# Reordering evictions, moving two norms and packing narrow products in a one-core encoder step

## The chip, the core and the metric

The kernel runs on one core of one Trainium2 chip. The core has a matrix engine (TensorE, "PE" in the profile, with its weight loads as "PEld"), VectorE ("DVE"), ScalarE ("ACT"), GpSimd ("POOL") and SyncE ("SP"), which issues nearly all of the kernel's DMAs. Each engine works through its own queue in order. The metric is the device time of one execution in microseconds (us); lower is better.

## What is computed

One layer of a streaming encoder, for a prompt of 2048 tokens and for a decoding batch of 8 sequences of 16 tokens (128 rows), both through the same weights. Width 1024, all in float32:

```python
qm, km, vm, om, ip, fp, qa, ka, va = split_in(x @ w_in)
hm, C1, n1, m1 = mlstm_chunkwise(qm, km, vm, logi, logf, C0, n0, m0, mchunk)   # 4 heads x 128
hm = og * head_norm(hm, g_mlstm_norm)
ha = swa_prompt(rope(qa), rope(ka), va, sinks)   # batch: swa_step, with a cache of 128 rows
mix = jnp.concatenate([hm, ha], axis=-1) @ w_out
h = layer_norm(DEEPNORM_ALPHA * x + mix, ln1_g, ln1_b)
u = h @ w_up                                     # 5632 columns: value | gate
c = b_conv + sum(ext[:, j:j + T] * w_conv[j] for j in range(CONV_W))
f = (silu(g) * a) @ w_down
y = layer_norm(DEEPNORM_ALPHA * h + f, ln2_g, ln2_b)
```

The mLSTM keeps a matrix state C and a vector n for each head; a token's numerator is the inner product within its chunk plus its query times the state. The prompt starts from C = 0; each of the 8 batch sequences brings its own state. The new states, the last keys and values and the last convolution rows are outputs too.

## The kernel before

The 2048 prompt tokens are 16 tiles of 128 rows (tiles 0 to 15); the batch is tile 16. Large products are made at near float32 accuracy from single-pass products: each operand is split into a high part (a cast on ACT, L217 for weights, L564 for tokens) and a low part (a subtraction on DVE, L218 and L565), and three products high x high, high x low, low x high are summed in PSUM. Blocks of the matrices are combined by a seven-product scheme of Strassen's kind, so a "step" s is one of seven products, and each step ends in an eviction out of PSUM that copies or adds. The splits for later steps run some steps ahead of their products.

PE's instructions run in exactly the order in which the program writes them. For the other engines and the DMA queues a planner fixes the order at compile time: from estimated durations it goes through a simulated time and gives each engine, of what is ready, the instruction with the highest priority, by default the one that the program wrote first. What the planner has put in a queue then runs in that order on the chip.

There are four stages in time.

1. **Input projection** (`i_dense`, to about 650 us). For four blocks of tiles and five column groups it runs `i_product` (L702, steps), `i_direct` (L728, gates, keys and values) and after each step `i_after`, which evicts (L769 on ACT, L773 and L775 on DVE are typical) and, through `i_out`, applies the rotary angles (`rope`, four DVE operations, L866 to L869, in group 2) and stores the result. `advance` then issues loads and splits for weights. Small chains are woven between the dense products: the batch (`t_sample`, `swa_sample`), the prompt's mLSTM tile by tile (`m_chain`, `m_tile`) and its attention (`a_chain`, `swa`). A chain is a generator: `yield cost, wait, banks` tells the weaver how much PE time its last part takes and how many ns of PE time are to pass before its next part is written into PE's stream. That wait is the lead which the chain's DVE, ACT and DMA work gets. `m_rows` sends gate rows through DRAM to all partitions (`wi<-zM`), and `m_tile` masks them on DVE (L1106).
2. **Output projection** (`o_block`, five blocks: tiles 16,0,1 / 2-5 / 6-9 / 10-13 / 14,15). An eviction adds the product to alpha * x (L1610), and the finished tile gets its first layer norm by the generator `norm` (statistics at L1564 and L1554, then two DVE operations over 1024 columns, L1568 and L1570, and the store to `zh`). The norms of one block advance on every second product of the next. Within the last block the up-projection already begins: `f_hT(0)` loads and transposes normed tiles (L1698), `f_tokens` splits them, `f_next` splits weights. The norms of the last block's own tiles 14 and 15 are made later, in the up-projection, by `o_late`.
3. **Up-projection** (`f_ups`, about 920 to 1861 us). Three blocks of tiles, 22 column pairs j each, seven steps (L1834). `f_after` does a step's eviction (L1851 to L1870) and, after steps 3 and 4, the convolution (L1882 on ACT, L1884 on DVE), the gate and the stores. `o_late` advances at steps 6 and 5 from j = 2 on; `f_hT` for the next block starts at j = 6 and advances at the same steps.
4. **Down-projection** (`f_downs`, to the end). Products at L2039; `add` evicts (L2066, L2068), then the second norm and the output.

For the batch, `t_sample` multiplies each head's queries with 8 states: per head 8 products of 128 stationary columns, of which only one sequence's 16 are not zero (`qm` holds them on a block diagonal, L1436), against 129 columns of state (L1439). `swa_sample` handles the 8 sequences in two halves; a half's products with the cached values (L1525) and the new values (L1526) go, for each of two kv heads, into a bank of 64 partitions, and each bank is evicted by itself (L1527).

Of the kernel before, what the change touches and what calls it, by code (L numbers as in the profile page):

```python
# [14 lines left out]
P = 128  # L15
# [189 lines left out]
class Prog:  # L205
# [380 lines left out]
    def i_dense(self):  # L586
# [34 lines left out]
        for item in self.items:  # L621
# [39 lines left out]
            behind = self.i_after(b, g, s)  # L661
# [378 lines left out]
    def m_chain(self):  # L1040
        nc = self.nc
        while not self.chains.done["s"]:
            yield 0, 500
        load = self.m_next = None
        for t in range(NPT):
            b, ti = self.place(t)
            while self.i_done <= b:
                yield 0, 500
            load = load or self.m_load(t, b, ti)
            if self.m_next is None:  # L1050
                self.m_next = self.m_rows(t, b, ti)
# [12 lines left out]
        nc.sync.dma_start(self.a["m_p"], self.mc)  # L1064
        nc.sync.dma_start(self.a["cn_p"], self.C)
# [116 lines left out]
    def m_tile(self, t, load):  # L1182
# [61 lines left out]
    def a_chain(self):  # L1244
# [115 lines left out]
    def t_sample(self):  # L1360
# [49 lines left out]
        qm = [self.work("sc", [P, DB * P], bufs=2, name="qm") for i in range(2)]  # L1410
# [16 lines left out]
        for j in range(2):  # L1427
            ps = self.bank([P, 2, 129], "pnum")
            for i in range(2):
# [5 lines left out]
                dg = bass.AP(q.tensor, q.offset, [list(q.ap[0]), [P + DS, DB], [1, DS]])  # L1435
                V.tensor_copy(dg, b3(qw[:, h]))  # L1436
                nc.tensor.matmul(ps[:, i], sd[:, h], v1[:, h], start=True, stop=False)
                for bb in range(DB):
                    nc.tensor.matmul(ps[:, i], q[:, bb * P:(bb + 1) * P], cn[:, bb], start=False, stop=bb == DB - 1)  # L1439
# [7 lines left out]
                yield 4000, 3500  # L1447
# [21 lines left out]
    def swa_sample(self, load, kvc):  # L1469
# [15 lines left out]
        for half in range(2):  # L1485
# [35 lines left out]
            for kvh in range(2):  # L1521
                po = self.bank([64, HB, 64], "ppo")
                cs = slice(64 * kvh, 64 * kvh + 64)
                for b in range(HB):
                    nc.tensor.matmul(po[:, b], vc[:, b, cs], pts[:, 0, b, cs], start=True, stop=False)  # L1525
                    nc.tensor.matmul(po[:, b], vn[:, b, cs], pts[:DS, 1, b, cs], start=False, stop=True)  # L1526
                (V.tensor_copy if kvh else nc.scalar.copy)(  # L1527
                    mix[cs].rearrange("p j (b l) -> p j b l", b=DB)[:, :, bs], po.rearrange("p b (j l) -> p j b l", j=4))
            if half == 0:
                kvc = self.swa_cache(1)  # L1530
            yield 1900, 500 if half else 7000
# [54 lines left out]
    def o_block(self, b):  # L1586
# [7 lines left out]
        for hf in range(2):  # L1594
            c = slice(hf * 512, hf * 512 + 512)
            steps = 0
            for cost, ti, ps in self.group(b, tiles, 8 * b + 4 * hf, hf == 1):
# [12 lines left out]
                nc.vector.scalar_tensor_tensor(y[:, c], ys[ti][:, c], ALPHA, ps, op0=ALU.mult, op1=ALU.add)  # L1610
                if hf and b < nb - 1:
# [11 lines left out]
    def o_late(self):  # L1623

        nc, V = self.nc, self.nc.vector
        st = []
        for y, t in self.late:
            st.append(self.stats(y))
            yield
        for hf in range(2):  # L1630
            c = slice(hf * 512, hf * 512 + 512)
            gb = self.f3.tile([P, 2, 512], F32, name="lnp", tag="th", bufs=1)
            for i, n in enumerate(("ln1_g", "ln1_b")):
                nc.sync.dma_start(gb[:, i], self.a[n][:, c].to_broadcast([P, 512]))
            yield
            yield
            for (y, t), (mv, s) in zip(self.late, st):
                V.scalar_tensor_tensor(y[:, c], y[:, c], mv[:, 0:1], gb[:, 0], op0=ALU.subtract, op1=ALU.mult)
                V.scalar_tensor_tensor(y[:, c], y[:, c], s[:, 0:1], gb[:, 1], op0=ALU.mult, op1=ALU.add)
                if hf:  # L1640
                    nc.sync.dma_start(self.zh[t], y)
                yield

# [135 lines left out]
    def f_ups(self, n):  # L1779
# [11 lines left out]
        for i, (b, j, s) in enumerate(self.seq):  # L1791
            if s == 6 and j == 6 and b + 1 < nb:
# [13 lines left out]
            if b + 1 < nb and j == NFF - 1:  # L1806
                if s == 1:
# [28 lines left out]
    def f_after(self, b, j, s):  # L1836
# [11 lines left out]
        m = WP - h  # L1848
        half = lambda v: f2.tile([P, 770], F32, name=f"u{v}", tag=f"u{v}", bufs=1)
# [19 lines left out]
        elif s == 4:  # L1869
            V.tensor_add(self.ug[:, 2:2 + h], C, self.u2[j % 2])  # L1870
        if s not in (3, 4):
            return

# [132 lines left out]
    def f_downs(self):  # L2006
# [35 lines left out]
        def after(s, p):  # L2042
            ps = banks[role[s][2 if p == np_ else p]]
            ta, tb = (tiles[2 * np_], None) if p == np_ else (tiles[p], tiles[np_ + p])
            if s == 1:
                S.copy(banks[role[6][2 if p == np_ else p]], ps)
# [16 lines left out]
        def add(t, half, ps, first):  # L2063
            y = ys[t][:, half * 512:half * 512 + 512]
            if first:
                V.scalar_tensor_tensor(y, y, ALPHA, ps, op0=ALU.mult, op1=ALU.add)  # L2066
            else:
                V.tensor_add(y, y, ps)  # L2068
# [71 lines left out]
```

## Time and profile before

| | |
|---|---|
| median of 3 runs | 2336.47 us (2332.86 to 2341.85) |
| profiled execution | 2337.74 us, of which the span from the first to the last instruction is 2336.0 us |
| mean granted TensorE clock | 0.992 of full speed |
| DMA | 629.24 MB, mean 269 GB/s |

| stretch, us | stage | PE busy | DVE busy | ACT busy |
|---|---|---|---|---|
| 0 to 900 | input and output projection | 883.90 | 688.12 | 537.87 |
| 900 to 940 | last output block, start of the up-projection | 35.02 | 39.68 | 23.19 |
| 940 to 1860 | up-projection | 916.13 | 706.60 | 511.48 |
| 1860 to 2336 | down-projection | 465.46 | 384.26 | 202.66 |

A row of the timeline gives the start in us, the duration, engine, line, operation, "out<-in", for a matmul the size of its stationary operand (128*128) and of its moving one (128x256), and the count; in brackets stands the idle time of the engine before it and what ended that. The row of an x2 or x4 covers that many instructions up to the last one's end. A matmul's duration contains its way through the array, so the distance of two starts tells what it costs in a stream. The page's busy time counts an engine as busy while any of its instructions is under way, at whatever clock.

### The profile page before, as it was taken

The numbers are of one execution on the slowest core, as the hardware profiler recorded it, in microseconds if no ns is written. First come the engines' busy times: TensorE is split into PE (matmuls) and PEld (weight loads), VectorE is DVE, ScalarE is ACT, GpSimd is POOL, SyncE is SP. The second block draws the span as 40 slices with busy tenths as digits, with TensorE's granted clock in tenths as the row PEclk, the third lists the DMA queues.
The fourth block names the chain that finished last, engine by engine and source line by source line (L and its number), as shares of the span: only waits on it lengthen the run. The fifth ranks groups of instructions, "written<-read, shape, count | busy, mean of one in ns | idle before, by whom it ended". The sixth has DMA issues, their size and how long they took to land. (4 is left out here: it accounts for less than half of the span.)

```text
span 2336.0 us, 39880 instructions
## 1 busy us (share of the span) xinstructions
PE 2300.5 (98%) x14301; PEld 2112.0 (90%) x14301; DVE 1818.7 (78%) x3187; ACT 1275.2 (55%) x2409; POOL 253.0 (11%) x477
## 2 busy tenths in 40 slices
PE   8999999999999999999999999999999999999998
PEld 8999989998987777999999999999999978888876
DVE  7786587797688888988788776778766786896987
ACT  5453457776766664556556555556554544444452
POOL 0001000000011111211102010102111200100100
PEclk9999999999999999999999999999999999999999
DMA  7888889989987766788777889878998786756753
GB/s 271 293 304 294 285 271 337 318 291 330 327 274 251 233 214 250 268 319 295 265 275 267 311 310 318 304 266 279 308 299 262 224 288 197 258 175 226 251 157 108
DMA packets 298727, 629.24 MB, mean 269 GB/s; under 512 B 47709, under 2 KB 140961, under 8 KB 298529
## 3 DMA queue, kind: packets, MB, share of 16 engines
q1 hardware_dynamic: 294144, 612.99, 76.7%
q0 software_dynamic: 3520, 10.56, 1.4%
q10 hardware_dynamic: 864, 3.15, 0.3%
q8 instruction: 113, 1.85, 0.3%
q14 instruction: 86, 0.70, 0.1%
HBM read 456.01 MB, written 170.59 MB: 268 GB/s over the span
## 5 line engine op out<-in xcount | busy, mean ns | idle before, releaser
L1834 PE MATMUL fup<-hh,uw 128*128 128x384 f32 (+1 forms) x1848 | 480.7, 329 | 2.5 <-DVE uw L218 2.1
L1834 PE MATMUL dps<-hh,uw 128*128 128x384 f32 (+1 forms) x1848 | 478.7, 328 | 3.4 <-DVE u L1864 2.4
L1834 PEld LDWEIGHTS fup<-hh,uw 128*128 128x128 f32 x1848 | 331.6, 189 | 3.7 <-DVE uw L218 2.4
L1834 PEld LDWEIGHTS dps<-hh,uw 128*128 128x128 f32 x1848 | 330.2, 188 | 4.2 <-DVE u L1864 2.7
L1884 DVE SCALAR_TENSOR_TENSOR cc<-u,cw,cc 128x768 f32<-128x768 f32 (+1 forms) x264 | 258.4, 979 | 63.8 <-ACT cc L1882 57.6
L1834 PE MATMUL fup<-hl,uw 128*128 128x384 f32 (+1 forms) x924 | 303.7, 329 | 2.6 <-DVE hl L218 2.5
L1834 PE MATMUL dps<-hl,uw 128*128 128x384 f32 (+1 forms) x924 | 302.5, 327 | 0.0
L702 PE MATMUL dps<-w,oh 128*128 128x256 f32 x1344 | 257.2, 286 | 1.3 <-DVE zev L775 0.8
L217 ACT CAST uw<-wraw 128x1024 fp32r<-128x1024 f32 x126 | 123.0, 979 | 225.5 <-PE dps L2039 119.9
L218 DVE TENSOR_TENSOR w<-wraw,w 128x1024 fp32r<-128x1024 f32 (+2 forms) x167 | 189.0, 1139 | 55.4 <-ACT w L217 54.3
L217 ACT CAST w<-wraw 128x1024 fp32r<-128x1024 f32 (+2 forms) x167 | 162.9, 983 | 119.1 <-PE dps L702 57.1
L702 PEld LDWEIGHTS dps<-w,oh 128*128 128x128 f32 x1344 | 212.5, 189 | 12.8 <-issue 8.9
L218 DVE TENSOR_TENSOR uw<-wraw,uw 128x1024 fp32r<-128x1024 f32 x126 | 142.3, 1131 | 66.2 <-ACT uw L217 66.0
L702 PE MATMUL dps<-w,ol 128*128 128x256 f32 x672 | 188.8, 281 | 0.0
L1834 PEld LDWEIGHTS fup<-hl,uw 128*128 128x128 f32 x924 | 174.5, 189 | 3.3 <-DVE hl L218 3.2
L2039 PE MATMUL fup<-uw,fu 128*128 128x512 f32 x726 | 174.5, 396 | 1.7 <-DVE uw L218 1.7
L702 PE MATMUL dps<-oh,w 128*128 128x256 f32 x896 | 170.7, 285 | 5.3 <-ACT zev L769 3.2
L1834 PEld LDWEIGHTS dps<-hl,uw 128*128 128x128 f32 x924 | 173.6, 188 | 0.0
L2039 PEld LDWEIGHTS fup<-uw,fu 128*128 128x128 f32 x726 | 136.8, 189 | 35.2 <-DVE uw L218 2.1
L2039 PE MATMUL dps<-uw,fu 128*128 128x512 f32 x660 | 165.2, 395 | 1.1 <-DVE uw L218 1.1
L1882 ACT ACTIVATE cc<-u,cw 128x768 f32<-128x768 f32 (+1 forms) x132 | 132.2, 1002 | 56.4 <-DVE u L1870 30.0
L702 PEld LDWEIGHTS dps<-oh,w 128*128 128x128 f32 x896 | 142.0, 191 | 11.9 <-issue 4.1
(323 smaller groups left out, 4594.7 us busy)
## 6 DMA issues: line engine op xcount, KB each, us to landing
uw<-zw SPq DMA_DIRECT2D x176, 512.0 KB, 5.3
zw<-uw SPq DMA_DIRECT2D x88, 512.0 KB, 2.9
w<-zws SPq DMA_DIRECT2D x72, 512.0 KB, 6.4
wv<-wup SPq DMA_DIRECT2D x66, 512.0 KB, 4.5
wraw<-wi SPq DMA_DIRECT2D x65, 512.0 KB, 5.1
wraw<-zt SPq DMA_DIRECT2D x60, 512.0 KB, 4.2
wraw<-wdn SPq DMA_DIRECT2D x45, 512.0 KB, 4.1
wraw<-wo SPq DMA_DIRECT2D x40, 512.0 KB, 4.8
```

What stands on the lines that cost most here:

```text
L217: nc.scalar.copy(hi, src)
L218: nc.vector.tensor_sub(lo, src, hi.bitcast(F32))
L702: mm(o, l, r, start=s in (1, 7) and c == k == i == 0, stop=k == 3 and i == 2, skip_group_check=True)
L1834: mm(ps, l[:, k], r[:, k], start=s in (1, 7) and k == 0 and i == 0, stop=k == 3 and i == 2, skip_group_check=True)
L1882: S.activation(c[:, v], u[:, 2:2 + n], AF.Identity, bias=w[3], scale=w[2])
L1884: V.scalar_tensor_tensor(c[:, v], u[:, i:i + n], w[i], c[:, v], op0=ALU.mult, op1=ALU.add)
L2039: mm(ps, l[:, k, c], r[:, k], start=s in (1, 4, 7) and u == 0 and k == 0 and i == 0, stop=u == nu - 1 and k == n - 1 and i == 2, skip_grou ...
```

## The change

Six edits:

1. **Priority.** The evictions of the input projection (all of `i_after`), of the output projection (L1610), of the up-projection (cut out of `f_after` as `f_evict`) and of the down-projection (`add`, and the copy of step 1) are written inside `high_priority()`: the planner takes them before any other instruction that is ready on that engine. PE's order is not touched by it.
2. **Longer leads.** At the first tile of an input block the mLSTM chain waits 15000 ns instead of 12000 after `m_rows`, the attention chain 9000 instead of 4500 after its load.
3. **Tile 0** of the prompt leaves out the product with the state C, which is zero there.
4. **State products of the batch.** The block diagonal `qm` shrinks from 128 to 32 columns per sequence; pairs of sequences share a group of 32 output partitions, and the loop goes over the four groups in turn. The part's cost is given as 2800 ns instead of 4000.
5. **Value products of the batch.** Both kv heads of a half go to one bank of 128 partitions, in neighbouring instructions, with one eviction. Cost 1000 instead of 1900.
6. **Norms of tiles 12 and 13.** Their un-normed rows are stored to `zh` at once; `o_late`, after tiles 14 and 15, loads them again, norms them and stores them. `o_late` advances at steps 6, 5 and 7, and `f_hT` of the next block starts at j = 12 instead of 6.

```diff
-            behind = self.i_after(b, g, s)
+            with self.tc.high_priority():
+                behind = self.i_after(b, g, s)
...
-                yield 150, 12000, 1
+                yield 150, 15000, 1
...
-                nc.tensor.matmul(ps[:, i], sd[:, h], v1[:, h], start=True, stop=False)
-                nc.tensor.matmul(ps[:, i], qk[:, h], self.C[:, h], start=False, stop=True)
+                nc.tensor.matmul(ps[:, i], sd[:, h], v1[:, h], start=True, stop=t == 0)
+                if t:
+                    nc.tensor.matmul(ps[:, i], qk[:, h], self.C[:, h], start=False, stop=True)
...
-                yield 0, 4500
+                yield 0, 9000
...
-                dg = bass.AP(q.tensor, q.offset, [list(q.ap[0]), [P + DS, DB], [1, DS]])
-                V.tensor_copy(dg, b3(qw[:, h]))
-                nc.tensor.matmul(ps[:, i], sd[:, h], v1[:, h], start=True, stop=False)
-                for bb in range(DB):
-                    nc.tensor.matmul(ps[:, i], q[:, bb * P:(bb + 1) * P], cn[:, bb], start=False, stop=bb == DB - 1)
+                dg = bass.AP(q.tensor, q.offset, [list(q.ap[0]), [64, DB // 2], [32 + DS, 2], [1, DS]])
+                V.tensor_copy(dg, qw[:, h].rearrange("p (c b l) -> p c b l", b=2, l=DS))
+                nc.tensor.matmul(ps[:, i], sd[:, h], v1[:, h], start=True, stop=False, skip_group_check=True)
+                for r in range(2):
+                    for c in range(DB // 2):
+                        nc.tensor.matmul(ps[32 * c:32 * c + 32, i], q[:, 2 * c + r], cn[:, 2 * c + r], start=False, stop=r == 1, skip_group_check=True)
...
-            for kvh in range(2):
-                po = self.bank([64, HB, 64], "ppo")
-                cs = slice(64 * kvh, 64 * kvh + 64)
-                for b in range(HB):
-                    nc.tensor.matmul(po[:, b], vc[:, b, cs], pts[:, 0, b, cs], start=True, stop=False)
-                    nc.tensor.matmul(po[:, b], vn[:, b, cs], pts[:DS, 1, b, cs], start=False, stop=True)
...
+            po = self.bank([P, HB, 64], "ppo")
+            for b in range(HB):
+                for i, (v, p) in enumerate(((vc[:, b], pts[:, 0, b]), (vn[:, b], pts[:DS, 1, b]))):
+                    for kvh in range(2):
+                        cs = slice(64 * kvh, 64 * kvh + 64)
+                        nc.tensor.matmul(po[cs, b], v[:, cs], p[:, cs], start=i == 0, stop=i == 1, skip_group_check=True)
...
+                if hf and b == nb - 2 and ti >= len(tiles) - 2:
+
+                    nc.sync.dma_start(self.zh[tiles[ti]], y)
+                elif hf and b < nb - 1:
                     self.norms.append(self.norm(y, *self.ln1, self.zh[tiles[ti]]))
...
+        for late in (self.late, OBLOCKS[-2][-2:]):
+            if late is not self.late:
+                late = [(self.fp.tile([P, D], F32, name="ymix", tag="hst", bufs=2), t) for t in late]
+                for y, t in late:
+                    nc.sync.dma_start(y, self.zh[t])
+                for _ in range(3):
+                    yield
...
-            if s == 6 and j == 6 and b + 1 < nb:
+            if s == 6 and j == 12 and b + 1 < nb:
...
+            with self.tc.high_priority():
+                self.f_evict(b, j, s)
             self.f_after(b, j, s)
...
-            if j >= 2 and s in (6, 5):
+            if j >= 2 and s in (6, 5, 7):
                 next(late, None)
...
+            with self.tc.high_priority():
+                if first:
+                    V.scalar_tensor_tensor(y, y, ALPHA, ps, op0=ALU.mult, op1=ALU.add)
+                else:
+                    V.tensor_add(y, y, ps)
```

More of the change, by code (lines that the diff above doesn't have):

```diff
@@ L1409, in t_sample @@
         states = [state(h) for h in range(2)]
-        qm = [self.work("sc", [P, DB * P], bufs=2, name="qm") for i in range(2)]
+        qm = [self.work("sc", [P, DB, 32], bufs=2, name="qm") for i in range(2)]
         for q in qm:
@@ L1446, in t_sample @@
                 vws = weighted(h + 1) if h + 1 < MH else None
-                yield 4000, 3500
+                yield 2800, 3500
             num.append(ps)
@@ L1609, in o_block @@
                 y = outs[ti]
-                nc.vector.scalar_tensor_tensor(y[:, c], ys[ti][:, c], ALPHA, ps, op0=ALU.mult, op1=ALU.add)
-                if hf and b < nb - 1:
+                with self.tc.high_priority():
+                    nc.vector.scalar_tensor_tensor(y[:, c], ys[ti][:, c], ALPHA, ps, op0=ALU.mult, op1=ALU.add)
+                if hf and b == nb - 2 and ti >= len(tiles) - 2:
+                    nc.sync.dma_start(self.zh[tiles[ti]], y)
+                elif hf and b < nb - 1:
                     self.norms.append(self.norm(y, *self.ln1, self.zh[tiles[ti]]))
@@ L1625, in o_late @@
         nc, V = self.nc, self.nc.vector
[L1626 to L1641, printed above, removed]
-                yield
+        for late in (self.late, OBLOCKS[-2][-2:]):
[5 more added lines that the diff above has]
+                    yield
+            st = []
+            for y, t in late:
+                st.append(self.stats(y))
+                yield
+            for hf in range(2):
+                c = slice(hf * 512, hf * 512 + 512)
+                gb = self.f3.tile([P, 2, 512], F32, name="lnp", tag="th", bufs=1)
+                for i, n in enumerate(("ln1_g", "ln1_b")):
+                    nc.sync.dma_start(gb[:, i], self.a[n][:, c].to_broadcast([P, 512]))
+                yield
+                yield
+                for (y, t), (mv, s) in zip(late, st):
+                    V.scalar_tensor_tensor(y[:, c], y[:, c], mv[:, 0:1], gb[:, 0], op0=ALU.subtract, op1=ALU.mult)
+                    V.scalar_tensor_tensor(y[:, c], y[:, c], s[:, 0:1], gb[:, 1], op0=ALU.mult, op1=ALU.add)
+                    if hf:
+                        nc.sync.dma_start(self.zh[t], y)
+                    yield
     def f_setup(self):
@@ L1806, in f_ups @@
             if b + 1 < nb and j == NFF - 1:
+                if s == 1 and b == 0:
+                    assert next(late, self) is self
                 if s == 1:
@@ L1848, in f_after @@
         m = WP - h
+        self.fshape = n, WP, has_s, sam
         half = lambda v: f2.tile([P, 770], F32, name=f"u{v}", tag=f"u{v}", bufs=1)
@@ L1870, in f_after @@
             V.tensor_add(self.ug[:, 2:2 + h], C, self.u2[j % 2])
+    def f_after(self, b, j, s):
         if s not in (3, 4):
             return
+        nc = self.nc
+        V, S = nc.vector, nc.scalar
+        n, WP, has_s, sam = self.fshape
         v, u = (0, self.uv) if s == 3 else (1, self.ug)
@@ L2045, in after @@
             if s == 1:
-                S.copy(banks[role[6][2 if p == np_ else p]], ps)
+                with self.tc.high_priority():
+                    S.copy(banks[role[6][2 if p == np_ else p]], ps)
             elif s == 2:
@@ L2064, in add @@
             y = ys[t][:, half * 512:half * 512 + 512]
[L2065 to L2068, printed above, removed]
+            with self.tc.high_priority():
+                if first:
+                    V.scalar_tensor_tensor(y, y, ALPHA, ps, op0=ALU.mult, op1=ALU.add)
+                else:
+                    V.tensor_add(y, y, ps)
         def finish(t, b, step):
```

7 lines of the change are left out of this document (3 added, 4 removed).

## The prediction

> **What bounds the kernel now.** Read first the page: the span and the busy time of each engine.
>
> ```profile
> span 2336.0 us, 39880 instructions
> PE 2300.5 (98%) x14301; PEld 2112.0 (90%) x14301; DVE 1818.7 (78%) x3187; ACT 1275.2 (55%) x2409; POOL 253.0 (11%) x477
> ```
>
> TensorE (PE) is idle for 35.5 us in all. No reordering of other engines can win more than that, except in two ways: PE gets fewer or cheaper matmuls, or its clock stays up. So the second view is the timeline of PE alone, for rows that carry idle time before them. After the first 50 us these are the ones that bear on this change (start, duration, engine, line, operation; in brackets the idle time and what ended it):
>
> ```profile
> 306.45 0.56 PE L728 MATMUL dps<-w,oh 128*128 128x264 f32 x2 [2.23 <-DVE zev L775]
> 334.27 0.58 PE L702 MATMUL dps<-oh,w 128*128 128x256 f32 x1 [2.49 <-ACT zev L769]
> 472.86 0.52 PE L728 MATMUL dps<-w,oh 128*128 128x264 f32 x2 [1.51 <-DVE zev L775]
> 584.16 0.39 PE L702 MATMUL dps<-w,oh 128*128 128x256 f32 x1 [0.78 <-DVE zev L775]
> 923.25 0.62 PE L1834 MATMUL fup<-hh,uw 128*128 128x384 f32 x2 [2.10 <-DVE uw L218]
> 933.92 0.44 PE L1834 MATMUL fup<-hl,uw 128*128 128x384 f32 x1 [2.49 <-DVE hl L218]
> 1588.34 0.44 PE L1834 MATMUL dps<-hh,uw 128*128 128x384 f32 x1 [0.60 <-DVE u L1862]
> 1858.70 0.42 PE L1834 MATMUL dps<-hh,uw 128*128 128x320 f32 x1 [2.44 <-DVE u L1864]
> ```
>
> Six of the eight wait for an eviction (L769, L775, L1862, L1864): DVE or ACT had other work in front. The other two wait for a split (L218). The third view is the table of stretches, because a stall can cost twice. Columns: stretch, length, then busy time of PE, PEld, DVE, ACT, POOL with instruction counts, then PEclk (granted clock, 1.00 is full), DMA share, GB/s.
>
> ```profile
> 262.60:266.00 3.40, 3.40 (x17) 2.81 (x18) 0.42 (x1) 0.00 (x0) 0.00 (x0) 0.50 0.39 137
> 266.00:269.40 3.40, 3.40 (x18) 3.40 (x18) 0.69 (x1) 1.18 (x2) 0.00 (x0) 0.52 0.23 76
> ...
> 286.50:289.90 3.40, 3.40 (x29) 2.73 (x28) 3.37 (x4) 2.54 (x5) 0.00 (x0) 1.00 0.93 285
> ...
> 306.90:310.40 3.50, 3.50 (x19) 3.50 (x19) 3.50 (x4) 1.05 (x1) 0.00 (x0) 0.53 0.72 224
> ...
> 334.30:337.70 3.40, 3.40 (x17) 3.40 (x18) 0.68 (x1) 1.33 (x2) 0.00 (x0) 0.53 0.97 346
> ...
> 474.80:478.20 3.40, 3.40 (x31) 3.40 (x30) 3.40 (x7) 3.02 (x5) 0.00 (x0) 1.00 0.66 212
> ...
> 924.80:928.20 3.40, 3.40 (x12) 3.40 (x12) 3.40 (x6) 0.46 (x1) 0.00 (x0) 0.53 0.71 286
> ...
> 935.00:938.40 3.40, 3.40 (x12) 3.31 (x11) 3.40 (x4) 2.66 (x6) 0.00 (x0) 0.52 0.52 203
> ...
> 1860.00:1863.40 3.40, 3.40 (x12) 2.93 (x11) 3.40 (x6) 0.93 (x1) 0.00 (x0) 0.52 0.52 181
> ```
>
> The reader is to see that after each idle time of 2.1 us or more the clock is granted at half for the next 3.4 us, and PE, though "busy", does half the work: 3.4 x 0.47 = 1.6 us lost. After the 1.51 us before 472.86 it stays at 1.00. So a stall of 2.1 us or more really costs 1.6 us more than it shows. The stretch from 262.6 has no idle time at all; it comes behind narrow matmuls, below.
>
> **Part 1: less and denser PE work.** The trace records each f32 product twice.
>
> ```profile
> 198.88 1.95 PE L1439 MATMUL pnum<-cns,qm 128*128 128x129 f32 x16
> 200.67 1.90 PE L1443 MATMUL pcs<-vws,kw 128*128 128x387 f32 x6
> ...
> 259.66 0.33 PE L1525 MATMUL ppo<-pts,kvc 128*64 128x64 f32 x2
> ...
> 264.10 0.47 PE L1526 MATMUL ppo<-pts,vn 16*64 16x64 f32 x2
> ...
> 287.71 0.33 PE L1525 MATMUL ppo<-pts,kvc 128*64 128x64 f32 x2
> ...
> 291.55 0.32 PE L1526 MATMUL ppo<-pts,vn 16*64 16x64 f32 x2
> ```
> ```profile
> 350.12 0.65 PE L1349 MATMUL ppo<-pth,kva 128*64 128x512 f32 x2
> 350.60 0.60 PE L1349 MATMUL ppo<-pth,kva 128*64 128x512 f32 x2
> ```
> ```profile
> 274.57 0.44 PE L1498 MATMUL pscs<-kvc,qs 64*64 64x128 f32 x4
> 274.84 0.25 PE L1499 MATMUL pscs<-ks,qs 64*64 64x16 f32 x4
> 274.93 0.43 PE L1498 MATMUL pscs<-kvc,qs 64*64 64x128 f32 x4
> ```
>
> The batch's state products (L1439) take 200.67 - 198.88 = 1.79 us a head, 16 records at 0.112. Tile 0's product with the zero state C has the same shape and goes: four heads, two records each, 8 x 0.112 = 0.9 us.
>
> L1439's become 16 records of 32 columns in four column groups. If nothing overlaps, nothing is gained; if all four do, 1.79 / 4 = 0.45 is left. That groups overlap here is shown by L1349: two 64-column products start together, and the next two 0.48 us later. The nearest row for a pace is L1498: from 274.57 to 274.93 eight records (four of L1498, four of L1499) go, 0.045 us each. 16 x 0.045 = 0.72, and up to 0.26 for changing the array's shape before and after (no more than a whole product of L1525 takes, next paragraph): about 1.0. Saving 0.8 x 4 = 3.2 us; ends 0 and 5.4.
>
> The attention's L1525/L1526 took 287.71 to 291.81 = 4.1 us in the second half: 16 products in turn, (291.55 - 287.71) / 15 = 0.26 each, alternating between 128 and 16 rows. In the first half it was 259.66 to 264.50 = 4.8. Now both kv heads go to one bank, 64 columns each, with two products to every change of rows: 8 steps. I take 0.27 for a step, since L1349 shows pairs side by side: 2.2 us per half. Saving 2.6 + 1.9 = 4.5; none if a pair runs in turn. Of the two evictions one is left, off the path.
>
> The clock goes with it. From 259.66 to 262.6 there were 2.9 us of narrow products and the clock fell; the second half put 2.2 us of them into 286.5 to 289.9 and it didn't. 2.2 us is all that is left of a half, so the fall goes: 264.5 to 269.4 at half is 2.4 us. Part 1: 0.9 + 3.2 + 4.5 + 2.4 = **11.0 us**.
>
> The Trainium skill ("TensorE: Matmul & The Clock Gate", Part 3, on what overlaps) speaks against some of this: matmuls start and end strictly in program order. Then a product's second record would hold back the next group's first, and a head would need 8 x 0.112 + 0.26 = 1.2 us, an attention step about 0.05 more: 1.6 us less saved, 2313 in place of the forecast below. The L1349 rows speak for pairs that start together, if the two started together are of different groups, which no column tells.
>
> **Part 2: evictions first, longer leads, in the input projection.** 2.23 + 2.49 + 1.51 + 0.78 = 7.0 us of idle time and two clock falls, 3.2 us. What stood in front of the first:
>
> ```profile
> 303.97 0.69 DVE L1106 TENSOR_TENSOR dt<-k_mcau,wi 128x512 f32<-128x512 f32 x1 [3.00 <-DMA wi<-zM]
> 304.58 1.22 DVE L565 TENSOR_TENSOR ol<-xr,oh 128x1024 fp32r<-128x1024 f32 x1
> ...
> 305.72 0.68 DVE L775 TENSOR_TENSOR zev<-dps,zev 128x512 f32<-128x512 f32 x1
> ```
>
> DVE, in order, sat 3.00 us on a mask whose broadcast had not landed, then did a split of 1.22 us, then the eviction. The lead of 15000 in place of 12000 moves the mask 3 us back, which is as long as it waited; the priority moves the split behind L775. Only one of the two is needed to bring this stall under 2.1 us. I take three quarters of the idle time, 5.3 us, and both falls: **8.5 us**; at most 10.2. The lead of 9000 for the attention's load acts once per input block; what it adds lies beside dense products, whose count is the same.
>
> **Part 3: two norms moved.**
>
> ```profile
> 898.75 0.69 DVE L1554 BATCH_NORM_STATS2 lst<-ymix 128x6 f32<-128x512 f32 x1
> ...
> 901.20 1.27 DVE L1568 SCALAR_TENSOR_TENSOR ymix<-ymix,lmv,o_ln_g 128x1024 f32<-128x1024 f32 x1
> ...
> 902.91 1.28 DVE L1570 SCALAR_TENSOR_TENSOR ymix<-ymix,lsc,o_ln_b 128x1024 f32<-128x1024 f32 x1 [0.31 <-POOL lsc L1557]
> ```
> ```profile
> 910.00:920.00 10.00, 10.00 (x45) 8.11 (x44) 10.00 (x11) 3.04 (x4) 0.00 (x0) 1.00 0.52 159
> ```
>
> A norm is 2 x 0.69 + 1.27 + 1.28 = 3.9 us of DVE, two are 7.9. DVE has no free moment from 910 on, so what follows comes up to 7.9 us sooner; the stalls at 923 and 934 want 2.10 and 4.6 together. Both go with their falls: 4.6 + 3.2 = 7.8. I take **7 us**, as some splits also wait for transposes. The moved norms bring two stores, two loads and four parameter loads on SP's queue, three yields behind their issue, and the same DVE time some 50 to 150 us later. Up to each moment DVE has then been given no more work than before, so its backlog isn't larger. The transposes of block 1 start six steps later and still end before the last step needs them. If this cover failed, 7.9 us would come back.
>
> **Part 4: evictions first, later stages.**
>
> ```profile
> 1856.82 0.89 DVE L1884 SCALAR_TENSOR_TENSOR cc<-u,cw,cc 128x656 f32<-128x656 f32 x1
> ```
>
> This and a split stood before L1862 and L1864 of the last step, from 1856.8 to 1858.1. Going first saves 1.3 of the 2.44 us, and the fall (1.6). With 0.5 of the 0.60 at 1588: **3.4 us**. In the down-projection the same priority finds little idle time to win.
>
> **Sum.** 11.0 + 8.5 + 7 + 3.4 = 29.9 us. Parts 2 to 4 redraw the order of DVE, ACT and SP; an order planned from estimates meets the chip with stalls of its own. I give back a quarter of their 19: 5 us. 25 us off the profiled execution's 2337.74 is 2312.7; the median of the runs shown is 1.3 below it: **2311.5**.
>
> **Rivals.**
> 1. The stalls only move: other splits or masks become late as L775 is served, and parts 2 and 4 net nothing. For it: the eight waits have five different releasers, so they look like chance. Against: PE waits for evictions in six. 11 + 7: 2318.5.
> 2. It doesn't do what it says: 32- and 64-column products still run in turn. Part 1 shrinks to 0.9, and the clock falls again: 25 - 10.1 = 14.9, so 2321.6. L1349 speaks against it. If the stalls move as well, only 0.9 + 7 is left: 2328.6.
> 3. Slower: the priority covers all of i_after, so the rotary work too, and splits wait for it.
>
> ```profile
> 250.79 0.42 DVE L866 TENSOR_TENSOR rb<-zev,ropet 128x256 f32<-128x256 f32 x1
> ...
> 251.65 0.69 DVE L868 TENSOR_TENSOR zev<-zev,ropet 128x512 f32<-128x512 f32 x1
> ```
>
> One rotary pass is 2 x 0.42 + 2 x 0.69 = 2.2 us of DVE, 16 passes (four per block in group 2) are 35 us. It decides where splits are less than 2.2 us ahead of their products. If all were, with parts 1 and 3 still won, 2336.5 + 35 - 18 = 2353. Against it: in the steady stretch PE waits for evictions, not for w.
>
> **How the numbers follow.** Forecast 0.55 (own range 2303 to 2320), rival 1 0.20, rival 2 0.10, rival 2 with moved stalls 0.08, rival 3 0.07. All gains at their upper ends and nothing given back reach 2301; with rivals 1 and 2 taken in the range is 2301 to 2327. A measurement tells 0.5% (11.7 us, 2324.8) from no change. Faster 0.78, within 0.15, slower 0.07.
>
> **What would show it.** L1439's line at 1.0 us a head; the two attention stretches at 2.2 us with PEclk 1.00 behind them; no idle time of 2 us or more at L702, L728 and L1834; DVE free time before 920. It would be wrong if PE's idle time came out near 35 us again, or if waits for w or uw by L218 grew.

## The result, and the profile after

| kernel | median | runs | ratio to the kernel before |
|---|---|---|---|
| before | 2335.15 us | 6 | |
| changed | 2322.59 us (2317.53 to 2328.13) | 6 | 0.9943 [0.9927, 0.9959] |
| changed, once more (e11) | 2321.53 us (2321.05 to 2324.56) | 5 | 0.9942 [0.9928, 0.9955] |

The change is worth 0.57%, 12.6 us, with the whole interval below 1: faster, but by half of the 25 us that were forecast. 2322.59 lies in the prediction's range of 2301 to 2327, which takes rivals 1 and 2 in, but not in the forecast's own, 2303 to 2320. Two rows of the changed kernel's page say where to look:

```profile
span 2322.7 us, 39853 instructions
...
PE 2287.1 (98%) x14293; PEld 2095.7 (90%) x14293; DVE 1818.9 (78%) x3189; ACT 1274.3 (55%) x2409; POOL 261.3 (11%) x477
```

PE's idle time is 2322.7 - 2287.1 = 35.6 us; before it was 35.5. So the part of the change that was meant to remove waits removed none in sum. All of the gain is in PE's busy time, 2300.5 - 2287.1 = 13.4 us. PE has 8 instructions less, the eight records of tile 0's product with the zero state; the rest of the 13.4 us are products that take less time, because they are narrower or because the clock stays up. From 20 us on to the down-projection's end, the profiled execution of before has eight windows of 3.41 us at half clock, that of the changed kernel three.

The waits are still there, at other places. These are the rows of PE's timeline in the changed kernel with the longest idle time ahead of them behind the first 50 us (columns as before):

```profile
329.79 0.58 PE L703 MATMUL dps<-oh,w 128*128 128x256 f32 x1 [3.56 <-ACT mr L1151]
...
685.92 1.53 PE L1345 MATMUL ppt<-ident,sc 128*128 128x128 f32 x6 [1.47 <-ACT sc L1323]
...
919.84 0.49 PE L1853 MATMUL fup<-hl,uw 128*128 128x384 f32 x1 [2.50 <-DVE hl L218]
...
1846.64 0.41 PE L1853 MATMUL dps<-hh,uw 128*128 128x320 f32 x1 [1.99 <-DVE u L1884]
...
1890.91 6.33 PE L2065 MATMUL fup<-uw,fu 128*128 128x512 f32 x26 [1.63 <-DVE uw L218]
```

The first row comes in place of the stalls at 306.45 and 334.27 of before, some 13 us further on in the stream than the second of them, and is longer than either. The one at 923.25 is gone, the one at 933.92 stays as 919.84 with the same 2.5 us, and the one at 1858.70 became 1.99. The wait of 1.47 us at 685.92 is new. The last row is no new one: the kernel before waits 1.66 us at the same place.

What stood ahead of the first stall is on DVE's timeline of the changed kernel, then on ACT's:

```profile
324.69 0.69 DVE L849 TENSOR_TENSOR txy<-txy 128x512 f32<-128x512 f32 x1 [3.45 <-DMA txy<-wdn]
325.30 0.29 DVE L1148 BATCH_NORM_STATS2 bst<-pnum 128x6 f32<-128x128 f32 x1
```
```profile
328.12 0.17 ACT L1151 ACTIVATE mr<-pnum 128x2 f32<-128x2 f32 x1 [2.69 <-DVE bst L1148]
328.20 1.04 ACT L217 CAST w<-wraw 128x1024 fp32r<-128x1024 f32 x1
329.15 0.59 ACT L770 ACTIVATE zev<-dps 128x512 f32<-128x512 f32 x1
```

DVE sat 3.45 us at the head of its queue on a load of the down-projection's weights (`wdn`, for sums that are made ahead of time). The mLSTM chain's statistics came late by that; ACT, in order as well, sat 2.69 us on them; and the eviction L770, which is now marked to go first, came out at 329.15, behind them and a cast. (The row of PE names the next `mr` on ACT; L770 ends at 329.74 and that one at 329.80, after PE has started.) This is the picture of before with other names: one engine waits at the head of its queue for a load, and PE waits at the end of the row.

To see where the 13 us arise, each of the 12097 dense matmuls of the changed kernel was laid beside the one with the same number in the kernel before. What the changed kernel gains on each stretch (times of before, us):

| stretch | what lies there | gained |
|---|---|---|
| 0 to 45 | start; a half-clock stretch at 40.5 is missing | 2.0 |
| 45 to 193 | steady input projection | -1.3 |
| 193 to 237 | state products of the batch | 4.0 |
| 237 to 297 | value products, and the clock behind them | 6.3 |
| 297 to 341 | stalls at 306 and 334 with their half clock, tile 0's product | 7.2 |
| 341 to 358 | the changed kernel's own stall at 329.79 and its half clock | -5.6 |
| 358 to 650 | rest of the input projection | 1.9 |
| 650 to 903 | output projection: new stall and half clock at 686 | -4.5 |
| 903 to 952 | start of the up-projection, moved norms | 4.1 |
| 952 to 1841 | up-projection | -2.5 |
| 1841 to 1882 | last step of the up-projection | 2.0 |
| 1882 to the end | down-projection | -0.3 |

The packed products give 4.0 + 6.3 and tile 0's 0.9, 11.2 us; the norms 4.1; all the rest comes to -2.0. From about 300 to 470 us the chains stand at other places between the dense products, and the gain swings by up to 2.6 us from product to product; of the three rows from 297 to 650 only the sum, 3.5 us, is firm.

The table compares two executions, and some rows hold chance. e9 below has all six edits, and its clock is at half again from 40.7 us on, so the first 2.0 us are not the change's. e11 is the changed kernel once more: the same wait of 1.47 us in the output projection brings no half clock there, while its wait at the last step of the up-projection, 1.99 us as here, brings one there and none here.

The timeline of PE around the batch's products in the changed kernel:

```profile
198.00 0.38 PE L1440 MATMUL pnum<-v,sd 128*128 128x129 f32 x2
198.31 0.65 PE L1443 MATMUL pnum<-cns,qm 128*32 128x129 f32 x16
198.89 2.00 PE L1447 MATMUL pcs<-vws,kw 128*128 128x387 f32 x6
...
255.58 0.34 PE L1531 MATMUL ppo<-pts,kvc 128*64 128x64 f32 x4
...
257.42 0.33 PE L1531 MATMUL ppo<-pts,vn 16*64 16x64 f32 x4
```

The 16 records of a head now take 198.89 - 198.31 = 0.58 us in the stream, against 1.79. The products ahead of them and behind them take 0.2 us more together than before (from 198.00 to 198.31 it is 0.31 us, where it was 0.22), so a head saves 1.0 us. A half of the value products has eight steps, (257.42 - 255.58) / 7 = 0.263 us each, 2.1 us in all, against 4.8 and 4.1. And the clock, in the table of stretches of the changed kernel (columns as in the prediction):

```profile
254.50:257.90 3.40, 3.40 (x44) 2.72 (x42) 1.56 (x2) 1.30 (x3) 0.00 (x0) 1.00 0.92 344
257.90:261.30 3.40, 3.40 (x31) 3.40 (x31) 0.69 (x1) 1.45 (x3) 0.00 (x0) 1.00 0.76 213
```

It stays at 1.00 behind the narrow products, where it was 0.50 and 0.52 before.

### The profile page after: what moved, and what is told of

The parts are those of the page before. It is cut to its first block, busy times and chain, and to the rows that moved or that the text cites. A ratio compares the mean times of both kernels' runs of the same rounds, so it can differ in the third digit from the quotient of the medians.

```text
span 2322.7 us, 39853 instructions
## 1 busy us (share of the span) xinstructions
PE 2287.1 (98%) x14293; PEld 2095.7 (90%) x14293; DVE 1818.9 (78%) x3189; ACT 1274.3 (55%) x2409; POOL 261.3 (11%) x477
```

## The experiments

Four theories went into them. **A**: the gain is the packing's and part of the norms'; the priority and the leads move stalls and remove none. **B**: the priority removes waits, as forecast. **C**, formed after the first four: packing pays only with the attention chain's longer lead. **D**, formed for e7: the stalls that are left come from the written order, a load of down-projection weights issued too shortly ahead of its sums, and weight sums of the up-projection written ahead of the split `hl`; writing these differently takes the waits away. None of the kernels leaves out part of the computation; e9 makes one product three times.

**e1: the packing alone** (edits 3, 4 and 5 in the kernel before; the core of it):

```diff
-                    nc.tensor.matmul(ps[:, i], q[:, bb * P:(bb + 1) * P], cn[:, bb], start=False, stop=bb == DB - 1)
+                        nc.tensor.matmul(ps[32 * c:32 * c + 32, i], q[:, 2 * c + r], cn[:, 2 * c + r], start=False, stop=r == 1, skip_group_check=True)
...
-            yield 1900, 500 if half else 7000
+            yield 1000, 500 if half else 7000
```

> The kernel before with edits 3, 4 and 5 alone (tile 0's product left out, packed state and value products). Theory A (the narrow products and the clock that they cost are nearly the whole gain; the priority only moves stalls): 12 us less than before, ratio 0.995, no fall of the clock behind the value products. Theory B (every part pays as the forecast's terms say): 11 us less. If the packed products ran in turn, 1 us less and the clock falls again.

Measured: 2335.25 us (11 runs), 0.9994 [0.9983, 1.0005]. Nothing, although the products are as short as in the changed kernel. PE's timeline of e1 shows who took the gain:

```profile
292.01 1.09 PE L1240 MATMUL pq<-ident,qa 128*128 128x128 f32 x4 [3.65 <-DMA qa<-zqa]
```

With the batch's products shorter, the next chain is reached sooner, and its load of `qa` has not landed. 3.65 us of idle time, with half clock from 291.0 to 297.8 behind it, eat most of what was won. Laid beside the kernel before, e1 leads by 9.6 us ahead of this place and by 3.1 behind it, and by 2.1 at 400 us.

**e2: the priority alone** (edit 1 in the kernel before):

```diff
-            behind = self.i_after(b, g, s)
+            with self.tc.high_priority():
+                behind = self.i_after(b, g, s)
...
+            with self.tc.high_priority():
+                self.f_evict(b, j, s)
```

> The kernel before with edit 1 alone (all evictions first). Theory A: within 3 us of before, PE's idle time again 33 to 38 us, at other places. Theory B: 9 to 12 us less than before, idle time below 29 us.

Measured: 2340.32 us (12 runs), 1.0021 [1.0013, 1.003]: slightly slower. Against B. At the place from which the forecast was made the mark does what was said. DVE's timeline of e2:

```profile
303.63 0.69 DVE L1107 TENSOR_TENSOR dt<-k_mcau,wi 128x512 f32<-128x512 f32 x1 [0.96 <-DMA wi<-zM]
304.24 0.68 DVE L776 TENSOR_TENSOR zev<-dps,zev 128x512 f32<-128x512 f32 x1
304.84 1.22 DVE L565 TENSOR_TENSOR ol<-xr,oh 128x1024 fp32r<-128x1024 f32 x1
```

The eviction comes ahead of the split, and PE's wait of 2.23 us there is gone. But PE waits elsewhere: 2.27 us at 257.34, 3.85 at 334.48, 1.47 at 699.86 and 3.70 at 935.89 (2.49 before). In all it is idle for 39.4 us, where before it was 35.5. PE's timeline of e2 at the longest of these waits, then ACT's:

```profile
334.48 0.58 PE L703 MATMUL dps<-oh,w 128*128 128x256 f32 x1 [3.85 <-ACT zev L770]
```
```profile
331.73 1.28 ACT L1322 ACTIVATE sc<-sc,asm 128x128 f32<-128x128 f32 x4 [0.50 <-DVE asm L1320]
332.91 1.03 ACT L217 CAST w<-wraw 128x1024 fp32r<-128x1024 f32 x1
333.85 0.59 ACT L770 ACTIVATE zev<-dps 128x512 f32<-128x512 f32 x1
```

PE had finished the step at 330.6 and waited for nothing but this eviction. Marked or not, it stands behind an activation of the attention chain and a cast. The order of the queue was fixed at compile time, and a mark there only chooses among what the planner holds ready at that moment of its own time; that it thought PE later than it was here fits, but is argued, not measured.

**e3: the norms alone** (edit 6 in the kernel before; the core of it):

```diff
+                if hf and b == nb - 2 and ti >= len(tiles) - 2:
+
+                    nc.sync.dma_start(self.zh[tiles[ti]], y)
...
-            if j >= 2 and s in (6, 5):
+            if j >= 2 and s in (6, 5, 7):
```

> The kernel before with edit 6 alone (norms of tiles 12 and 13 moved). Theory A: 4 us less than before, since of the two stalls at the start of the up-projection one stays. Theory B: 7 us less, both stalls gone.

Measured: 2332.19 us (12 runs), 0.9986 [0.9976, 0.9995], 3.3 us: A's size, not the forecast's 7. One of the two stalls stays. PE's timeline of e3, and DVE's ahead of it:

```profile
930.00 0.69 PE L1850 MATMUL fup<-hl,uw 128*128 128x384 f32 x1 [2.66 <-DVE hl L218]
```
```profile
924.58 0.69 DVE L1769 TENSOR_TENSOR uw<-wg 128x512 f32<-128x512 f32 x1
925.19 0.69 DVE L1770 TENSOR_TENSOR uw<-wv,wg 128x512 f32<-128x512 f32 x1
925.79 0.69 DVE L1771 TENSOR_TENSOR uw<-uw,wv 128x512 f32<-128x512 f32 x1
926.39 0.68 DVE L218 TENSOR_TENSOR uw<-uw 128x512 fp32r<-128x512 f32 x1
926.99 0.68 DVE L1772 TENSOR_TENSOR uw<-wv,uw 128x512 f32<-128x512 f32 x1
927.59 0.69 DVE L218 TENSOR_TENSOR uw<-wv,uw 128x512 fp32r<-128x512 f32 x1
928.20 1.75 DVE L218 TENSOR_TENSOR hl<-hraw,hh 128x1536 fp32r<-128x1536 f32 x1
```

The norms are gone from here, but the split `hl` has four sums of weights (L1769 to L1772) and two weight splits ahead of it, 3.6 us from the first one's start to its own, all written earlier by the program.

**e4: the changed kernel without the priority** (all five places):

```diff
-            with self.tc.high_priority():
+            with nullcontext():
```

> The changed kernel without edit 1 (no priority, everything else). Theory A: within 3 us of the changed kernel's 2322.6. Theory B: 9 to 12 us more than it, 2332 to 2335.

Measured: 2322.79 us (6 runs), 0.9946 [0.9931, 0.996], the changed kernel's time. Its PE waits 1.08 us at 327.13, where the changed kernel's waits 3.56, but 1.93 at 502.22 and 2.45 at 1840.43, where the changed kernel's waits not at all and 1.99. The stalls at 306 and 334 of before are gone here too, without any mark. With e2 this settles edit 1: it is worth nothing that these runs can tell, and their intervals leave some 0.15% to either side. The wait of 1.47 us in the output projection even comes with it: of the fourteen kept traces (one execution of before, of the changed kernel and of each experiment) the five with marks on its evictions (changed, e2, e8, e9, e11) have it, and none of the other nine.

**e5: the packing with the attention lead** (e1 and):

```diff
-                yield 0, 4500
+                yield 0, 9000
```

> The kernel e1_narrow with one number more: the attention chain waits 9000 instead of 4500 after its load. Theory C (packing brings about 11 us, but makes the batch's chain end sooner, so that the prompt's attention starts on a load that has not landed; that stall and its clock fall eat 7 us of it): the stall of 3.65 us on qa<-zqa and the fall behind it are gone, 7 to 11 us less than before. Rival (the missing gain lies elsewhere, or the mLSTM chain's lead is the one that counts): within 4 us of before.

Measured: 2325.97 us (6 runs), 0.9957 [0.9945, 0.9969]: 10.1 us, and no wait on `qa` is left. C holds. With the 3.3 us of e3 that makes 13.4, and the changed kernel has 12.6: within the intervals these two parts account for the gain.

**e6: both leads alone** (edit 2 in the kernel before):

```diff
-                yield 150, 12000, 1
+                yield 150, 15000, 1
...
-                yield 0, 4500
+                yield 0, 9000
```

> The kernel before with edit 2 alone (both leads longer). Theory C: there is no late qa load in the kernel before, so little to win; the stall of 2.23 us behind the mask that waits for wi<-zM goes with its clock fall: 2 to 5 us less. Rival (the leads are the real gain, whatever the products): 8 us or more less.

Measured: 2334.39 us (10 runs), 0.9995 [0.9986, 1.0003]. By themselves the leads are worth nothing, and the stall that they were to relieve is longer: 3.36 us at 307.12 instead of 2.23, behind a mask that waits 4.39 us for `wi` (L1106) instead of 3.00. The one at 334 is gone. Together with e1 and e5: 0 and 0 apart, 10 together (e5 has the attention lead alone of the two).

**e7: three places written differently** (against the changed kernel):

```diff
-                steps = (6, 2, 5) if g == last - 1 else (6, 5, 3)
+                steps = (6, 2, 5) if g == last - 1 else (6, 3, 4)
...
+        self.f_tokens(0, 2)
         for _ in range(AHEAD - n):
             self.f_next()
...
         self.banks = [[pool.tile([P, 512], F32, name=n, tag=n) for _ in range(3)] for pool, n in ((self.fup, "fup"), (self.dps, "dps"))]
-        self.f_tokens(0, 2)
...
-            with self.tc.high_priority():
+            with self.tc.high_priority() if (b, j) == (nb - 1, NFF - 1) else nullcontext():
                 self.f_evict(b, j, s)
```

The first edit leaves one step more between the load of `wdn` and the sums that DVE makes of it. The moved line makes the tokens of step 2 (the late `hl`); `f_next` makes weight sums. The priority stays at the last column pair of the up-projection alone; its four other places are undone (not shown).

> The changed kernel with priority only for the evictions of the up-projection's last step, the sums on the down weights (L849 to L852) one step later behind their load, and the split of the tokens of step 2 ahead of the first weight sums of j = 1. Theory D (what is left are heads of DVE's queue that wait or work for something else, not the rank of evictions): the stalls at the fourth product of the up-projection (2.5 to 2.7 us) and at its end (2.0 to 2.5) shrink below 1.5 us, no DVE wait on txy over 2 us; 4 to 8 us less than the changed kernel, 2315 to 2319. Rival (stalls only move): within 3 us of 2322.6.

Measured: 2319.37 us (6 runs, 2316.74 to 2320.89), 0.9926 [0.9915, 0.9937], 3.2 us below the changed kernel. PE's timeline of e7 in the input projection, at the start of the up-projection, and at its last step:

```profile
327.48 0.38 PE L702 MATMUL dps<-oh,w 128*128 128x256 f32 x1 [1.29 <-ACT zev L769]
...
916.85 0.44 PE L1851 MATMUL fup<-hl,uw 128*128 128x384 f32 x1 [1.45 <-DVE hl L218]
...
1842.09 0.63 PE L1851 MATMUL dps<-hh,uw 128*128 128x320 f32 x1 [2.43 <-DVE u L1882]
```

The wait of 3.56 is one of 1.29, and the wait for `hl` fell from 2.50 to 1.45; the half clock went from both. That agrees with D, clearly for `hl`; at 327 the kernel of e4 waits as little (1.08 us) with the old steps, so there the cause isn't told apart. D's other signs fail: DVE still waits 2.73 and 2.84 us for loads of `wdn` (L849 at 391.15 and L848 at 498.90), and 3.2 us is less than the 4 that it asked for. The one place with the priority kept its stall. DVE's timeline of e7 there:

```profile
1838.26 0.89 DVE L1908 SCALAR_TENSOR_TENSOR cc<-u,cw,cc 128x656 f32<-128x656 f32 x1
1839.07 1.22 DVE L218 TENSOR_TENSOR uw<-wraw,uw 128x1024 fp32r<-128x1024 f32 x1
1840.20 0.89 DVE L1908 SCALAR_TENSOR_TENSOR cc<-u,cw,cc 128x656 f32<-128x656 f32 x1
1841.02 0.55 DVE L218 TENSOR_TENSOR fu<-r,fu 128x384 fp32r<-128x384 f32 x1
1841.48 0.35 DVE L1880 TENSOR_TENSOR u<-dps,ub 128x192 f32<-128x192 f32 x1
1841.75 0.28 DVE L1882 TENSOR_TENSOR u<-dps,ub 128x128 f32<-128x128 f32 x1
```

**e12: e7 without that last priority** (in its place `nullcontext()`).

> The kernel of e7 (split steps (6,3,4), batch tiles' transposes two steps earlier) without the last priority that e7 kept, that of the up-projection's final step. Theory D, by which e7's gain over the changed kernel comes from the splits standing away from the weight sums: 2319 +- 2 again, ratio 0.991 to 0.994, the stall at the first down products' hand-over 2.4 us as in e7, the stall on hl at the start of the up-projection at most 1.6 us. Rival, by which the priority held that last step together or e7's 3 us were spread of the runs: 2322 or more, ratio 0.9945 or above, or the last stall over 3 us with a fall of the clock longer than one 3.4 us stretch.

Measured: 2322.12 us (6 runs, 2316.22 to 2328.03) beside a kernel before of 2338.51 on that chip, 0.9931 [0.9909, 0.9953]. By the ratio it is e7 again, by the median alone it isn't; the kernel before ran 2 to 3 us longer there too. DVE's timeline of e12 at the same place:

```profile
1841.95 0.35 DVE L1880 TENSOR_TENSOR u<-dps,ub 128x192 f32<-128x192 f32 x1
1842.21 0.28 DVE L1882 TENSOR_TENSOR u<-dps,ub 128x128 f32<-128x128 f32 x1
```

The same instructions in the same order (the four ahead of these too), 0.46 us later, and PE waits 2.43 us in both. Laid side by side, the queues of the two kernels differ in one pair of neighbours on DVE that change places (L1888 and L1934) and in nothing else on any engine; the pair stands at 1845.5, behind this wait. So in the last column pair the mark moved one eviction by one place, and not the one that PE waits for. e7 and e12 are in effect two measurements of one order: 0.9926 and 0.9931, against 0.9943, 0.9942 and 0.9946 for the changed kernel, the same again and e4. The gain of some 0.1% is of the size of the intervals; what is shown is the shorter wait.

**e10: DVE's work behind the last step's eviction** (e7, with an order in place of the priority):

```diff
+            behind = lambda: self.tc.issue_after(self.added) if final else nullcontext()
+            with behind():
+                self.f_after(b, j, s)
```

> e7_three_places, but in place of priority the DVE work written after the eviction of step 5 of the last column pair is queued behind that eviction. Theory E (priority ranks only what the planner holds ready, and the planner's PE is later than the chip's, so the rank does not help; a fixed order does): the stall of 2.43 us at the up-projection's end falls below 1 us, with no clock fall behind it, 1.5 to 3 us less than e7_three_places. Rival (DVE is simply full there): the stall stays or comes back at the first down products, within 1 us.

Measured: 2323.05 us (6 runs), 0.9947 [0.9933, 0.9961]. Now the eviction does come first and no wait is left at the last step, but the time is no better. PE's timeline of e10 some 22 us on:

```profile
1864.40 5.77 PE L2066 MATMUL fup<-uw,fu 128*128 128x512 f32 x17 [3.55 <-ACT fht L2073]
```

PE waits there for a copy out of PSUM, which ACT makes. ACT's timeline of e10:

```profile
1859.01 1.70 ACT L217 CAST fu<-r 128x768 fp32r<-128x768 f32 x2 [3.38 <-DMA r<-zf]
...
1863.77 1.06 ACT L2073 COPY fht<-fup 128x512 f32<-128x512 f32 x2
```

The copy stands behind casts of the down-projection's operands, and the first of those waited 3.38 us for its load. So 2.43 us saved come back as 3.55, once more behind a load at the head of a queue. Whether the work that the eviction overtook made that load late isn't shown.

**e11: the changed kernel once more**, on the chip of e9 and e10.

> The changed kernel itself once more, beside e10 on the same chip: 2320 to 2325. Theory D (heads of queues, not ranks): e10 is 4 us or more below it. Rival (stalls only move): less than 3 us between them.

Measured: 2321.53 us (5 runs), 0.9942 [0.9928, 0.9955], as in the first measurement. e10 is 1.5 us above it, not 4 below: D's sign fails and the rival's holds.

**e8: the group loop outside** (against the changed kernel; records of one column group now follow each other):

```diff
-                for r in range(2):
-                    for c in range(DB // 2):
+                for c in range(DB // 2):
+                    for r in range(2):
```

> The changed kernel with the two loops of the state products swapped: a column group's four records come one behind the other, then the next group's. If every matmul must start behind the one before it in the program, groups overlap only at their ends: 16 x 0.107 less three overlaps, about 1.4 us from L1443 to L1447. If each column group takes its records as soon as it is free, 0.58 us as in the changed kernel (198.31 to 198.89).

Measured: 2322.61 us (one run). PE's timeline of e8:

```profile
198.15 0.67 PE L1443 MATMUL pnum<-cns,qm 128*32 128x129 f32 x16
198.75 2.00 PE L1447 MATMUL pcs<-vws,kw 128*128 128x387 f32 x6
```

0.60 us instead of 0.58: the order of the groups hardly matters.

**e9: the value products three times** (against the changed kernel):

```diff
-            for b in range(HB):
+            for b in [*range(HB)] * 3:
```

> The changed kernel with each half's value products made three times over (every pass starts its sums anew, so the last one gives the result): 6.3 us of narrow products in a row in place of 2.1. If narrowness for longer than one 3.4 us window is what takes the clock down, PEclk falls to about 0.5 inside or right behind both stretches, and the second half too, which did not fall in the kernel before. If packed pairs keep the array busy enough, the clock stays at 1.00 and only 8.4 us are added.

Measured: 2336.34 us (one run; the changed kernel 2322.59). 24 steps of 0.263 us are 6.3 us for each half at full clock. The stretches in and behind them in e9:

```profile
261.30:264.70 3.40, 3.40 (x44) 2.46 (x41) 0.00 (x0) 0.00 (x0) 0.00 (x0) 0.68 0.45 127
264.70:268.10 3.40, 3.40 (x23) 3.07 (x20) 0.00 (x0) 0.37 (x1) 0.00 (x0) 0.50 0.20 44
...
291.20:294.60 3.40, 3.40 (x50) 2.48 (x46) 1.90 (x3) 0.54 (x2) 0.00 (x0) 0.81 0.99 287
```

The clock falls again, in both halves, and PE is never idle there. So the length of the narrow stretch takes the clock down, and the cut to 2.1 us is what keeps it up.

## Why the prediction was half right

The sign and the mechanism of Part 1 held; the forecast was 11 us too low, and its text named the sign of that in advance: it would be wrong "if PE's idle time came out near 35 us again". It did, at 35.6. The range holds the result because rivals 1 and 2 were taken in. The time nearest to it, 2321.6, is rival 2's, and that is luck: its mechanism, narrow products that run in turn, is what the runs refute. Step by step:

- **Part 1 (11.0): right.** 11.2 us by the matched matmuls. By rows: tile 0's product 0.9; a head 1.0 saved where 0.8 was put (the sixteen records need 0.58 us and their neighbours 0.2 more, 0.8 in place of 1.0, since the pace of L1498 was too slow a neighbour); the value products 2.7 + 2.0 where 2.6 + 1.9 was put; the clock as said. One thing was missing: it needs edit 2's lead for the attention chain. The prediction priced the lead of 9000 at nothing; without it packing gains 0 (e1), with it 10 (e5).
- **Part 2 (8.5): wrong, and the step that failed is "I take three quarters of the idle time, 5.3 us, and both falls".** That "the priority moves the split behind L775" held in e2. That the lead alone would do did not: in e6 the mask waits longer than before. The two stalls at 306 and 334 did go, with their falls, and they did so without the priority too (e4). But idle time that goes at one place was counted as gone for good: one wait of 3.56 us came some 13 us further on in the stream, and with the priority one of 1.47, here with a fall, in the output projection. Alone, the priority gives +0.2% (e2) and the leads nothing (e6); the priority taken away costs nothing (e4). Rival 1, stalls that only move, was the mechanism, at 2318.5; it had a chance of 0.20, and its time is nearer than the forecast's.
- **Part 3 (7): right in kind, too large.** 4.1 us by the matched matmuls, 3.3 alone (e3). "Both go with their falls" failed: one went, and the wait for `hl` stayed with its fall, 2.50 us at 919.84. DVE's time was freed, but `hl` stands behind weight sums in an order that the program wrote (moved ahead of them in e7, it costs 1.45). Between 890 and 897 us DVE of the changed kernel even waits 0.88, 1.23 and 1.03 us, and `hl` is late all the same.
- **Part 4 (3.4): wrong; the step that failed is "Going first saves 1.3 of the 2.44 us, and the fall (1.6)".** The wait at 1846 is 1.99 us instead of 2.44, so the mark saved 0.45 there. No fall followed in this execution, but one did in e11, behind the same wait in the same kernel. 2.0 us at this step stand against 2.5 lost on the way through the up-projection (1.1 in e11). In the kernels of e7 and e12 the mark left the decisive eviction where it was; e10 shows that forcing it moves the wait on.
- **"I give back a quarter of their 19"** was the sum's allowance for new stalls. By the matched matmuls parts 2 to 4 gave 13.3 - 11.2 = 2.1 of 19, and 2.0 of that is the half clock missing at 40.5, which is not the change's.
- Rival 2 (groups in turn) and rival 3 (slower) were rightly put low. The Trainium skill ("TensorE: Matmul & The Clock Gate", Part 3) states a strict order of starts and ends. By the prediction's working from it a head would be at 1.2 us; the runs have 0.58 and, in the order that should suffer most, 0.60. So that working doesn't hold here; in which order the records of different groups start isn't shown, since no column names the group.

What stays open: whether the planner's time has PE later than the chip does, which would explain why the marks don't take hold; what made the load late in e10; and whether e7's 2 to 3 us over the changed kernel are real.

## What to carry to other kernels

Where the busiest engine stands at 98%, fewer and shorter instructions on it are a gain that can be counted beforehand; a reordering of the other engines must be judged by the sum of its idle time, since a stall taken away is soon replaced by the next engine that sits at the head of its queue. When a part of the stream gets shorter, look for the load that was timed by its old length, and lengthen that lead in the same edit: neither edit is worth anything alone. A priority only chooses among what the planner holds ready; before trusting it, look in the trace whether the marked instruction has moved at all, and what waits in its place. And a fall of the clock that one execution shows can be missing in the next one of the same kernel; look at two before counting it.

## What the runs showed of the hardware

- Four groups of 32 columns ran side by side: 16 records of 129 columns in 0.58 us, 0.036 each, against 0.112 for full-width ones, in either order of the groups (e8: 0.60).
- The half clock needs no idle time: 6.3 us of 64-column products brought it in both halves (e9). 2.1 us did not, in any of the nine kept traces with the packed products made once.
- The waiting time by itself doesn't set it either. The Trainium skill ("TensorE: Matmul & The Clock Gate", Why this matters for your kernels) asks for no gaps over about 3 us; here a wait of 1.47 us was followed by a fall, though not in every execution. The table of stretches of the changed kernel, behind that wait:

```profile
688.00:692.00 4.00, 4.00 (x12) 3.09 (x12) 2.99 (x7) 2.01 (x7) 1.46 (x2) 0.57 0.93 355
```

- What counts is how much of the wait falls into one window of a fixed grid. In each of the fourteen kept traces all changes of the granted clock lie whole multiples of 3.413 us apart (to within 0.004 us), and the grid lies elsewhere in each execution. The tables of e7 and of e12 on their grids, around the wait of 2.43 us at the same step:

```profile
1838.32:1841.73 3.41, 1.34 (x10) 1.07 (x8) 3.41 (x6) 2.41 (x6) 1.66 (x5) 1.00 0.64 171
1841.73:1845.14 3.41, 3.05 (x11) 3.06 (x12) 2.73 (x5) 0.86 (x2) 1.13 (x4) 0.50 0.69 256
```
```profile
1837.86:1841.27 3.41, 2.25 (x16) 1.99 (x14) 3.41 (x5) 2.41 (x6) 1.66 (x3) 1.00 0.51 154
1841.27:1844.68 3.41, 2.13 (x14) 2.09 (x15) 3.41 (x7) 1.79 (x3) 2.06 (x5) 1.00 0.68 213
```

In e7 one window holds 3.41 - 1.34 = 2.07 us of the wait, and the next is at half clock. In e12 the same wait is cut into 1.16 and 1.28 us, and the clock stays up. Counted over all fourteen traces behind the first 50 us, each of the 34 full-clock windows with 1.97 us or more of idle time was followed by half clock. With 1.48 to 1.94 us 7 of 24 were, and with less than that only windows with narrow products, which have no idle time at all. The prediction's threshold of 2.1 us, for a wait wherever it lies, was drawn from too few rows. A fall costs 3.41 x 0.5 = 1.7 us where PE has work throughout, so this can be part of why runs of one kernel spread over 10 us.
